# Row sums on one core: the head of the stream as two blocks of neighbouring rows with stores of their own, and the last group loaded whole

## The chip, the cores and the metric

The kernel runs on one core of a Trainium2 chip. The metric is the device time of one execution in microseconds (us), as the median of several runs. Three kinds of engine matter here. SyncE (SP) issues the loads and the last store. VectorE (DVE) and ScalarE (ACT) add the rows up, and ScalarE also issues stores. The core's 16 DMA engines move all the data.

## The reference

```python
x = np.random.randn(32, 512, 1024).astype(np.float32)

def reference(x):
    return np.sum(x, axis=-1).astype(np.float32)
```

There are 16384 rows of 1024 float32 numbers (67.1 MB in all), and each row gives one sum (64 KB in all).

## The kernel before

The rows are laid over 128 partitions, so a partition handles 128 rows. They are cut into eight groups (`last` = 7 is the number of the last one) of 2048 rows: in a group, partition p has 16 neighbouring rows, `BIG` = 16, so 64 KB of consecutive memory. The tile `sums` has 128 partitions and 128 columns, one column for each row of a partition. Column `j` belongs to group `j // 16`.

Input tiles come from a pool of three buffers. A load into a buffer waits until the sums of what was in it are done.

The work is in this order, written out by hand (`manual_schedule`):

1. The first 7 rows per partition of the *last* group are loaded into the first tile (`FIRST`, line 199). This load is moved to the very entry of the program by `issue_first_load_at_entry`. One DVE instruction (`vec`, line 141) makes its 7 sums. That instruction is named `first`.
2. Groups 0 to 6 follow, 16 rows per partition in one load each (lines 201 to 208). Groups 0 to 5 are summed by one DVE instruction each. Of group 6, DVE sums 9 rows one by one (`halves`, line 155: it adds the two halves of a row and accumulates) and ScalarE 7 (`act`, line 168). The load of group 1 is held until `first` is done (line 208).
3. The other 9 rows of the last group come in falling pieces: 6 rows (4 on DVE, 2 on ScalarE), 2 rows (one on each; the load is named `two`), and one row in two pieces of 560 and 464 numbers (`pieces`), both on DVE (lines 210 to 226).
4. ScalarE's queue issues one store of the sums of groups 0 to 6 (line 224), held until the load `two` has landed. SP issues the store of the last group's sums at the very end (line 227).

Two more helpers act when the program is finished. `order_waits` sets which of several waits comes first in an instruction. `wait_for_the_store_at_the_clear` takes the wait for the last store by SP out of SP's waits at the end of the program and puts it on GpSimd's clearing of the semaphores; SP's waits for all other DMAs, ScalarE's store among them, stay where they are, ahead of the engines' last meeting.

Of the kernel before, what the change touches and what calls it, by code (L numbers as in the profile page):

```python
# [100 lines left out]
@with_exitstack  # L101
def kernel(
    ctx: ExitStack,
    tc: tile.TileContext,
    x: bass.AP,
    out: bass.AP,
):
    nc = tc.nc
    nc.at_finalize(issue_first_load_at_entry)
    nc.at_finalize(order_waits)  # L110
    nc.at_finalize(wait_for_the_store_at_the_clear)
    fp32 = mybir.dt.float32
    P = 128
    batch, seq, dim = x.shape
    rows = batch * seq
    J = rows // P
    BIG = 16


    x_g = x.flatten_outer_dims().rearrange("(g p j) d -> g p j d", p=P, j=BIG)  # L120
    out_v = out.rearrange("b s -> (b s)").rearrange("(g p j) -> p g j", p=P, j=BIG)

    def rows_from(j, n):
        return x_g[j // BIG, :, j % BIG : j % BIG + n, :]

    last = J // BIG - 1
    FIRST = 7
    pieces = (560, 464)  # L130

    with (
        tc.tile_pool(name="in", bufs=3) as inpool,
        tc.tile_pool(name="unread", bufs=4, space=bass.MemoryType.PSUM) as upool,
        tc.tile_pool(name="stage", bufs=1) as stpool,
        tc.manual_schedule(),
    ):
        sums = stpool.tile([P, J], fp32)

        def vec(dst, src):  # L140
            return nc.vector.tensor_reduce(  # L141
                out=dst, in_=src, axis=mybir.AxisListType.X, op=mybir.AluOpType.add
            )

        def hold(inst, until, reason):
            tc.add_manual_dep(
                inst.ins,
                until.ins.name,
                mybir.DependencyInfo(mybir.DependencyClass.Sync, mybir.DependencyReason.DATA),
                reason=reason,  # L150
            )

        def halves(dst, src):
            n = src.shape[-1] // 2
            return nc.vector.tensor_tensor_reduce(  # L155
                out=src[:, :n],
                in0=src[:, :n],
                in1=src[:, n:],
                scale=1.0,
                scalar=0.0,  # L160
                op0=mybir.AluOpType.add,
                op1=mybir.AluOpType.add,
                accum_out=dst,
            )

        def act(dst, src, n):
            unread = upool.tile([P, dim], fp32)
            nc.scalar.activation(  # L168
                out=unread[:, :n],
                in_=src,  # L170
                func=mybir.ActivationFunctionType.Copy,
                accum_out=dst,
            )

        sums_of = []

        def rows(t, a, n, j, n_act, pairs=False):
            nv = n - n_act
            block = t[:, a * dim : (a + n) * dim].rearrange("p (n d) -> p n d", d=dim)
            load = nc.sync.dma_start(out=block, in_=rows_from(j, n))  # L180
            if pairs:
                for q in range(nv):
                    sums_of.append(halves(sums[:, j + q : j + q + 1], block[:, q, :]))
            else:
                sums_of.append(vec(sums[:, j : j + nv], block[:, :nv, :]))
            for q in range(nv, n):
                act(sums[:, j + q : j + q + 1], block[:, q, :], dim)
            return load

        def store(eng, g0, g1):  # L190
            return eng.dma_start(
                out=out_v[:, g0:g1],
                in_=sums[:, g0 * BIG : g1 * BIG].rearrange("p (g j) -> p g j", j=BIG),
            )


        j = last * BIG
        t = inpool.tile([P, BIG * dim + 4], fp32)
        rows(t, 0, FIRST, j, 0)
        first = sums_of[-1]  # L200
        for g in range(last):
            t = inpool.tile([P, BIG * dim + 4], fp32)
            if g < last - 1:
                load = rows(t, 0, BIG, g * BIG, 0)
            else:
                rows(t, 0, BIG, g * BIG, 7, pairs=True)
            if g == 1:
                hold(load, first, "no descriptors of later loads while the first ones start")

        t = inpool.tile([P, BIG * dim + 4], fp32)  # L210
        rows(t, FIRST, 6, j + FIRST, 2, pairs=True)
        two = rows(t, FIRST + 6, 2, j + FIRST + 6, 1, pairs=True)
        a = BIG - 1

        j += a
        c, width = pieces
        whole = t[:, a * dim + c : BIG * dim + 2]
        nc.vector.memset(whole[:, width + 1 :], 0.0)  # L220
        part = t[:, a * dim : a * dim + c]
        nc.sync.dma_start(out=part, in_=rows_from(j, 1)[:, 0, :c])  # L222
        nc.sync.dma_start(out=whole[:, 1 : width + 1], in_=rows_from(j, 1)[:, 0, c:])
        hold(store(nc.scalar, 0, last), two, "its packets come behind those of the loads")
        halves(whole[:, :1], part)
        halves(sums[:, j : j + 1], whole)
        store(nc.sync, last, last + 1)


# [28 lines left out]
```

## Time and profile before

| what | value |
|---|---|
| device time, median of 3 runs | 161.91 us (161.54 to 161.96) |
| span of the profiled execution, first to last instruction | 159.9 us |
| DVE busy | 120.6 us (75%) |
| ScalarE busy | 12.0 us (8%) |
| DMA queue of SP (q1): packets, bytes, share of the 16 engines' span | 1872, 67.12 MB, 97.7% |
| DMA queue of ScalarE (q10): the same | 912, 0.06 MB, 0.4% |

The profile is of one execution, and it gives that execution's span only, not a device time of its own. The median of the runs is 2.0 us above the span; those 2.0 us lie outside the first and the last instruction. Times within the profile are counted from the start of the span, which is the issue of the first load. "Landing" is when the semaphore of a DMA shows that all its data has arrived. A packet, in this kernel's DMAs, is what one partition gets or gives.

### The profile page before, as it was taken

What the parts mean: (1) busy time and instruction counts of PE and PEld (TensorE: products, weight loads), DVE (VectorE), ACT (ScalarE), POOL (GpSimd) and SP (SyncE); (2) the same over time, 40 slices, a digit from 0 to 9 for tenths busy, and PEclk for the clock granted to TensorE, in tenths of its full rate; (3) what the DMA queues carried; (4) which work ended last, traced back from release to release, by engine and by line L of the source; (5) the groups of instructions that cost most, each with busy time, mean ns of one, the idle gap of its engine ahead of it and who ended that gap; (6) DMA issues with size and microseconds to landing.
All of it is one profiled execution on the core that took longest, in us unless ns stands there. A gap on an engine that the chain in (4) does not pass through costs nothing.

```text
span 159.9 us, 132 instructions
## 1 busy us (share of the span) xinstructions
DVE 120.6 (75%) x40; ACT 12.0 (8%) x21; POOL 0.2 (0%) x4
## 2 busy tenths in 40 slices
DVE  0029600499985999779995899949999499994955
ACT  3000000000000000000000000000000000003993
POOL 0000000000000000000000000000000000000000
DMA  8899899799699699699699699799898996996994
GB/s 308 380 492 525 361 426 525 328 459 525 295 492 525 262 525 525 262 525 525 262 525 508 279 525 476 312 525 410 377 525 361 426 525 262 525 525 289 400 384 124
DMA packets 2784, 67.18 MB, mean 420 GB/s; under 512 B 1248, under 2 KB 1376, under 8 KB 1504
## 3 DMA queue, kind: packets, MB, share of 16 engines
q1 hardware_dynamic: 1872, 67.12, 97.7%
q10 hardware_dynamic: 912, 0.06, 0.4%
HBM read 67.11 MB, written 0.07 MB: 420 GB/s over the span
## 4 chain that ended last, share of the span: by engine, by line
DMA 71%; DVE 27%; SPq 1%; issue 0%; DVEq 0%
DMA t<-in_x_dram 71%; DVE sums L141 26%; SPq L180 0%; SPq L222 0%; DVE t L155 0%; DVEq L253 0%
## 5 line engine op out<-in xcount | busy, mean ns | idle before, releaser
L141 DVE TENSOR_REDUCE sums<-t 128x16 f32<-128x16384 f32 (+1 forms) x7 | 110.9, 15848 | 33.4 <-DMA t<-in_x_dram 33.4
L168 ACT ACTIVATE unread<-t 128x1024 f32<-128x1024 f32 x10 | 10.1, 1013 | 144.7 <-DMA t<-in_x_dram 144.7
L155 DVE CUSTOM_DVE_ANT_0 t<-t 128x512 f32<-128x512 f32 (+2 forms) x16 | 9.6, 654 | 4.1 <-DMA t<-in_x_dram 4.0
L168 ACT ACTIVATION_READ_ACCUMULATOR unread<-t 128x1 f32 x10 | 1.9, 188 | 0.0
L168 ACT ACT_TABLE_LOAD x1 | 1.3, 1283 | 0.8 <-PEq L242 0.8
L155 DVE DVE_READ_ACCUMULATOR2_ANT sums<- 128x1 f32 x15 | 1.2, 81 | 0.0
L242 POOL MEMSET const-bfloat16-1.0<- 128x1 bf16 x1 | 0.1, 102 | 0.0
L242 POOL MEMSET const-uint8-127<- 128x1 uint8 x1 | 0.1, 102 | 0.0
L242 POOL MEMSET const-float32-1.0<- 128x1 f32 x1 | 0.1, 99 | 0.0
L242 POOL MEMSET const-float32-0.0<- 128x1 f32 x1 | 0.1, 98 | 0.2 <-issue 0.2
L155 DVE DVE_READ_ACCUMULATOR2_ANT t<- 128x1 f32 x1 | 0.1, 83 | 0.0
L220 DVE MEMSET t<- 128x1 f32 x1 | 0.1, 59 | 0.0
## 6 DMA issues: line engine op xcount, KB each, us to landing
t<-in_x_dram SPq DMA_DIRECT2D x1, 3584.0 KB, 11.0
t<-in_x_dram SPq DMA_DIRECT2D x1, 3072.0 KB, 28.9
t<-in_x_dram SPq DMA_DIRECT2D x1, 1024.0 KB, 31.0
t<-in_x_dram SPq DMA_DIRECT2D x1, 280.0 KB, 31.2
t<-in_x_dram SPq DMA_DIRECT2D x1, 232.0 KB, 31.3
t<-in_x_dram SPq DMA_DIRECT2D x7, 40.8
out_dram<-sums ACTq DMA_DIRECT2D x1, 56.0 KB, 2.1
out_dram<-sums SPq DMA_DIRECT2D x1, 8.0 KB, 1.4
```

What stands on the lines that cost most here:

```text
L141: return nc.vector.tensor_reduce(out=dst, in_=src, axis=mybir.AxisListType.X, op=mybir.AluOpType.add)
L155: return nc.vector.tensor_tensor_reduce(out=src[:, :n], in0=src[:, :n], in1=src[:, n:], scale=1.0, scalar=0.0, op0=mybir.AluOpType.add, op ...
L168: nc.scalar.activation(out=unread[:, :n], in_=src, func=mybir.ActivationFunctionType.Copy, accum_out=dst,)
L220: nc.vector.memset(whole[:, width + 1 :], 0.0)
L242: nc = _bacc.Bacc("TRN2", target_bir_lowering=False, num_devices=1)
```

## The change

Rows 0 to 2047 (what was group 0) become two blocks, each laid over the partitions by itself: rows 0 to 895 with 7 neighbouring rows per partition (`HEAD`), and rows 896 to 2047 with 9. Both are loaded first, into one tile, by two loads, and each is summed by one DVE instruction. ScalarE's queue stores the 7 sums and then the 9 sums of each partition, each as soon as they are there. Groups 1 to 6 are loaded and summed as before. The last group is now loaded whole at the end: in pieces of 8 rows (5 on DVE, 3 on ScalarE), 5 (3 and 2), 2 (1 and 1), and the one row in pieces of 560 and 464. The late store on ScalarE's queue has groups 1 to 6 alone. It is held until `two`, and `two` is now the DVE sum of the first of the two rows, where it was the load of both.

```diff
+    HEAD = 7
...
+    def block_of(j):
+        if j < HEAD:
+            return 0, HEAD
+        if j < BIG:
+            return HEAD, BIG - HEAD
+        return j // BIG * BIG, BIG
 
     def rows_from(j, n):
-        return x_g[j // BIG, :, j % BIG : j % BIG + n, :]
+        first, size = block_of(j)
+        block = x_r[first * P : (first + size) * P, :].rearrange("(p j) d -> p j d", j=size)
+        return block[:, j - first : j - first + n, :]
...
-            return load
+            return load, summed
...
+        def store_block(eng, j):
+            first, size = block_of(j)
+            return eng.dma_start(
+                out=out_r[first * P : (first + size) * P].rearrange("(p j) -> p j", j=size),
+                in_=sums[:, first : first + size],
+            )
...
-        j = last * BIG
         t = inpool.tile([P, BIG * dim + 4], fp32)
-        rows(t, 0, FIRST, j, 0)
-        first = sums_of[-1]
-        for g in range(last):
+        _, first = rows_in(t, 0, HEAD, 0, 0)
+        rows_in(t, HEAD, BIG - HEAD, HEAD, 0)
+        store_block(nc.scalar, 0)
+        store_block(nc.scalar, HEAD)
+        for g in range(1, last):
             t = inpool.tile([P, BIG * dim + 4], fp32)
             if g < last - 1:
-                load = rows(t, 0, BIG, g * BIG, 0)
+                load, _ = rows_in(t, 0, BIG, g * BIG, 0)
             else:
-                rows(t, 0, BIG, g * BIG, 7, pairs=True)
+                rows_in(t, 0, BIG, g * BIG, 7, pairs=True)
             if g == 1:
                 hold(load, first, "no descriptors of later loads while the first ones start")
 
         t = inpool.tile([P, BIG * dim + 4], fp32)
-        rows(t, FIRST, 6, j + FIRST, 2, pairs=True)
-        two = rows(t, FIRST + 6, 2, j + FIRST + 6, 1, pairs=True)
+        j = last * BIG
+        rows_in(t, 0, 8, j, 3, pairs=True)
+        rows_in(t, 8, 5, j + 8, 2, pairs=True)
+        _, two = rows_in(t, 13, 2, j + 13, 1, pairs=True)
...
-        hold(store(nc.scalar, 0, last), two, "its packets come behind those of the loads")
+        hold(
+            nc.scalar.dma_start(
+                out=out_r[BIG * P : last * BIG * P].rearrange("(g p j) -> p g j", p=P, j=BIG),
+                in_=sums[:, BIG : last * BIG].rearrange("p (g j) -> p g j", j=BIG),
+            ),
+            two,
+            "its packets come behind those of the loads",
+        )
         halves(whole[:, :1], part)
         halves(sums[:, j : j + 1], whole)
-        store(nc.sync, last, last + 1)
+        store_block(nc.sync, last * BIG)
```

More of the change, by code (lines that the diff above doesn't have):

```diff
@@ L117 @@
     BIG = 16
-    x_g = x.flatten_outer_dims().rearrange("(g p j) d -> g p j d", p=P, j=BIG)
-    out_v = out.rearrange("b s -> (b s)").rearrange("(g p j) -> p g j", p=P, j=BIG)
+    HEAD = 7
+    last = J // BIG - 1
+    pieces = (560, 464)
+    x_r = x.flatten_outer_dims()
+    out_r = out.rearrange("b s -> (b s)")
+    def block_of(j):
[4 more added lines that the diff above has]
+        return j // BIG * BIG, BIG
     def rows_from(j, n):
-        return x_g[j // BIG, :, j % BIG : j % BIG + n, :]
-    last = J // BIG - 1
-    FIRST = 7
-    pieces = (560, 464)
+        first, size = block_of(j)
+        block = x_r[first * P : (first + size) * P, :].rearrange("(p j) d -> p j d", j=size)
+        return block[:, j - first : j - first + n, :]
     with (
@@ L173, in act, with rows_in @@
             )
-        sums_of = []
-        def rows(t, a, n, j, n_act, pairs=False):
+        def rows_in(t, a, n, j, n_act, pairs=False):
             nv = n - n_act
@@ L182, in rows @@
                 for q in range(nv):
-                    sums_of.append(halves(sums[:, j + q : j + q + 1], block[:, q, :]))
+                    summed = halves(sums[:, j + q : j + q + 1], block[:, q, :])
             else:
-                sums_of.append(vec(sums[:, j : j + nv], block[:, :nv, :]))
+                summed = vec(sums[:, j : j + nv], block[:, :nv, :])
             for q in range(nv, n):
                 act(sums[:, j + q : j + q + 1], block[:, q, :], dim)
-            return load
-        def store(eng, g0, g1):
+            return load, summed
+        def store_block(eng, j):
+            first, size = block_of(j)
             return eng.dma_start(
-                out=out_v[:, g0:g1],
-                in_=sums[:, g0 * BIG : g1 * BIG].rearrange("p (g j) -> p g j", j=BIG),
+                out=out_r[first * P : (first + size) * P].rearrange("(p j) -> p j", j=size),
+                in_=sums[:, first : first + size],
             )
-        j = last * BIG
         t = inpool.tile([P, BIG * dim + 4], fp32)
-        rows(t, 0, FIRST, j, 0)
-        first = sums_of[-1]
-        for g in range(last):
+        _, first = rows_in(t, 0, HEAD, 0, 0)
[3 more added lines that the diff above has]
+        for g in range(1, last):
             t = inpool.tile([P, BIG * dim + 4], fp32)
             if g < last - 1:
-                load = rows(t, 0, BIG, g * BIG, 0)
+                load, _ = rows_in(t, 0, BIG, g * BIG, 0)
             else:
-                rows(t, 0, BIG, g * BIG, 7, pairs=True)
+                rows_in(t, 0, BIG, g * BIG, 7, pairs=True)
             if g == 1:
```

## The prediction

> **What bounds the kernel now.** I read the page first, for the share of the DMA queues; then the timeline around the loads' landings, to see whether the stream of loads ever pauses; then the trace's packet records, for the price of a packet; last the timeline and the instructions of the program's end.
>
> ```profile
> DVE 120.6 (75%) x40; ACT 12.0 (8%) x21; POOL 0.2 (0%) x4
> ...
> q1 hardware_dynamic: 1872, 67.12, 97.7%
> q10 hardware_dynamic: 912, 0.06, 0.4%
> ```
>
> The loads' queue (q1) keeps the 16 DMA engines busy for 97.7% of the span: the bytes bound this kernel, not DVE at 75%.
>
> ```profile
> 11.03 7.62 DVE L141 TENSOR_REDUCE sums<-t 128x7 f32<-128x7168 f32 x1 [11.03 <-DMA t<-in_x_dram]
> 30.34 17.22 DVE L141 TENSOR_REDUCE sums<-t 128x16 f32<-128x16384 f32 x1 [11.69 <-DMA t<-in_x_dram]
> 49.69 17.22 DVE L141 TENSOR_REDUCE sums<-t 128x16 f32<-128x16384 f32 x1 [2.14 <-DMA t<-in_x_dram]
> ...
> 127.09 17.22 DVE L141 TENSOR_REDUCE sums<-t 128x16 f32<-128x16384 f32 x1 [2.13 <-DMA t<-in_x_dram]
> ...
> 156.36 1.03 ACT L168 ACTIVATE unread<-t 128x1024 f32<-128x1024 f32 x1 [0.30 <-DMA t<-in_x_dram]
> 156.37 0.69 DVE L155 CUSTOM_DVE_ANT_0 t<-t 128x512 f32<-128x512 f32 x1
> 156.45 0.41 ACTq L191 DMA_DIRECT2D out_dram<-sums  x1
> 156.98 0.08 DVE L155 DVE_READ_ACCUMULATOR2_ANT sums<- 128x1 f32 x1
> ...
> 157.69 0.40 DVE L155 CUSTOM_DVE_ANT_0 t<-t 128x233 f32<-128x233 f32 x1
> 158.02 0.08 DVE L155 DVE_READ_ACCUMULATOR2_ANT sums<- 128x1 f32 x1
> 158.13 0.35 SPq L191 DMA_DIRECT2D out_dram<-sums  x1
> ```
>
> Columns: start, length, engine, line, what, and in brackets the idle time before it and what ended it. A new group starts every 19.35 us, also the very first one behind the 7 rows (30.34 - 11.03 = 19.31), and a group costs DVE 17.22, so DVE waits 2.13 each time: the stream has no pause from its first packet (1.02 us, by the packet records) to its last (157.24). Only three stretches can be shortened or lengthened by anything but bytes: the 1.02 before the first packet, the 2.6 after the last one, and whatever is put into the stream between.
>
> **The price of a packet.** By the trace's packet records a load packet of 65536 bytes takes 2418 ns, of 28672 bytes 1062, of 8192 bytes 309. The first two give 36864 bytes in 1356 ns, 27.19 bytes per ns, and 1062 - 28672 / 27.19 = 7.5 ns per packet on top. A DMA over 128 partitions gives each engine 8 packets and a semaphore packet of 9 ns. For the stores, the DMA view of the window from 157.3 to 158.3 us has ScalarE's store alone:
>
> ```profile
> DMA packets 912, 0.06 MB, mean 57 GB/s; under 512 B 912, under 2 KB 912, under 8 KB 912
> ...
> q10 hardware_dynamic: 912, 0.06, 56.4%
> ```
>
> 0.564 us on each of 16 engines for 912 packets is 9.9 ns a packet; from the first to the last, 157.40 to 158.13, it is 0.73 us for 57 per engine, 12.8 ns with the gaps.
>
> **Loads.** The bytes are the same; 12 loads become 13 (7, 9, six of 16, 8, 5, 2 and two parts of a row). One more load: 8 x 7.5 + 9 ns = **+0.07 us** in the stream.
>
> **The two early stores.** Each gives each engine 8 packets (28 and 36 bytes) and one semaphore packet. They come at about 19 and 32 us, in the middle of the stream, so what they occupy is added to it: 18 packets x 9.9 to 12.8 ns = 0.18 to 0.23, I take **+0.20 us**. Nothing in this trace shows a small store between large loads, so zero (it fits into gaps) and more (first rival) stay open. On ScalarE's queue they wait for DVE until 18.66 and about 31.7; behind them stand its table load, if it comes after them, and its first sum, due at about 138, so that wait is covered by 106 us.
>
> The Trainium skill speaks against this part: DMA: Bandwidth & Descriptors, Rules for kernel authors, says of many small transfers "Coalesce into one large transfer; under 64 KB you're paying mostly overhead", and its section on the anatomy of one DMA has a fixed cost of about 2.0 us for each (for DMAs from GpSimd). By that, three more DMAs would be +6 us if they stood in line. The rows above say that an engine is held for some 10 ns per packet, and the rest of the 1.4 us from the last store's issue to its landing is latency, for which nothing here waits.
>
> **The order of the head.** DVE gets its first 7 rows at 11.0 as before. The hold on the second 16-row load is released at 18.66 as before; what covers it is less: 9 rows instead of 16. Nine rows are 8 packets of 36864 bytes, 8 x (1356 + 7.5) = 10.91 us; the engines end the first load between 10.14 and 10.64, so they run dry between 21.05 and 21.55. Issued at 18.68, the held load's first packet comes 0.85 to 1.02 later by the other DMAs' rows (up to 1.55 on the last engine for the first load): 19.5 to 20.2. Margin 0.8 or more; cost nothing. If ScalarE's first store, released by the same sum, were served ahead of it, its 0.41 of issue leaves 0.4. Later the third 16-row load waits for the 9-row sum: landing at 21.9, 9.75 us of DVE (1.067 per row and 0.15, from 17.22 and 7.62), 31.7, while two loads, to about 60, are still queued. Cost nothing. The rest of the groups run 8.4 us earlier against the stream, each still faster than its load.
>
> **The tail.** Group 6 lands at about 138 and takes ScalarE 7 x 1.04; 8 rows later, 9.7 us, the next piece. 5 DVE sums x 0.615 end long before the 5 rows land (about 153.9, where the 6 rows did); 3 sums then end 0.6 before the 2 rows land, where 4 ended just with it. From there the chain is the same: the last piece's landing (157.62), 0.40 of sum, store, landing at 159.56. Nothing gained, since the landing already was the last to come.
>
> **The late store.** Its hold moves from the load `two` to a DVE sum of it, which ended at 157.06. With 0.03 from a DVE result to the issue (158.10 to 158.13) and up to 0.08 for ScalarE's own waits, it is issued at 157.09 to 157.17 instead of 156.45: +0.64 to +0.72, less 0.10 for 8 of 57 packets. It landed at 158.58, by the semaphore records, so now at 159.12 to 159.20. SP checks that semaphore in its round of waits at the end, at 158.60, second of five, just after the landing; so this cover is gone. From the check to the meeting's end was 0.62; then GpSimd clears the semaphores when the last store has landed, at 159.59. With the check in its old place the meeting would end at about 159.8 and the clear move by 0.2 to 0.3; as the last of the five checks (0.43 before the meeting's end) by 0.0 to 0.1. The order is not visible in this profile; I take the middle, **+0.15 us**.
>
> Sum: 0.07 + 0.20 + 0.15 = +0.42, on a span of 159.88 and so on the median: 161.91 + 0.42 = **162.33 us**, taking the 2.0 us outside the span as unchanged. With the low ends +0.26, with the high ones 0.07 + 0.23 + 0.30 = +0.60. About 0.3%, 0.49 us, is what a measurement of this kernel can tell from no change.
>
> **Rivals.**
> 1. *Switching* (slower). A small store between large loads may cost an engine not 10 ns a packet but a fresh start of its stream. Row: the first packets of the first load took 1673 ns on average, the next ones 1062, so a start costs 0.61. One start: 0.42 + 0.61 = +1.03, 162.9; one for each store: +1.64, 163.55. It decides from 0.07 us for both beyond my 0.20. For it: no row excludes it, as no store of this trace lies between loads. Against: the semaphore packets between two loads cost 9 ns and no start. Chance 0.17.
> 2. *The end's high side* (slower). The late store's check stays early in SP's round: the sum is +0.49 to +0.60, 162.45. Chance 0.21.
> 3. *Starving head* (slower). The held load's first packet needs over 2.4 us from its issue. Every us beyond costs one, and a start of 0.61: at 3 us, +0.42 + 0.6 + 0.6, 163.5. All three issue rows speak against it. Chance 0.05.
> 4. *Faster head.* Seven neighbouring rows in one stretch, instead of 28 KB out of each 64 KB, might read faster at the start: at most the 0.61 of the first packets, and with free stores and no late meeting 0.07 - 0.61 = -0.54, 161.4. Against: 24576-byte packets with the same 64 KB pitch took 912 ns, as the line above gives (911). Chance 0.07. [...]
> 5. *It does nothing.* Stores and end hidden: +0.07, 162.0, within 0.3%; chance 0.06.
>
> **How the numbers follow.** My forecast, the sum between +0.26 and +0.49, has 0.44 (its own range 162.1 to 162.4). Same is 0.44 + 0.06 = 0.50; slower 0.17 + 0.21 + 0.05 = 0.43; faster 0.07. The range reaches down to 161.8 (rival 5, and runs that differ by 0.4) and up to 163.3, between one and two starts; outside are rival 4 and the upper half of rivals 1 and 3, 0.07 + 0.11 = 0.18.
>
> **What would show it.** Right: loads still without a pause, the 16-row sums 19.35 apart, the first of them at about 41.3; the last piece landing at 157.8 to 158.0 (157.62 + 0.27); ScalarE's late store issued 0.6 to 0.7 after the `two` rows land; the clear 0.0 to 0.3 later against that landing. Wrong: a gap of the DMA engines near 21 us (rival 3), 16-row steps at 21 or 41 us longer by more than 0.3 (rival 1), a first landing before 10.7 (rival 4).

## The result and the profile after

The changed kernel takes 162.07 us (161.78 to 162.44, 9 runs), the kernel before 161.58 in 9 runs beside it (161.50 to 161.96). The ratio on record is 1.0025, with a 95% interval from 1.0015 to 1.0036: 0.40 us slower, between 0.24 and 0.58 (the two medians alone lie 0.49 apart). That is clear of zero. The estimate is below 0.3%, as forecast, but the interval reaches to 0.36%, and the prediction gave this 0.50 against 0.43 for slower. 162.07 lies in its range.

The base of the forecast was off. The three runs that the prediction started from had a median of 161.91; by the longer series before is at 161.6 to 161.7. The 2.0 us that the text before and the prediction put outside the span come from setting that median against the span of another execution: in every run here whose span is on record the time is 1.7 to 1.9 us above its own span. So the profile before, with its span of 159.88, belongs to a time of about 161.65, and 161.65 + 0.42 is 162.07.

The page of the changed kernel, its DMA queues (packets, MB, share of the 16 engines' span):

```profile
q1 hardware_dynamic: 2016, 67.12, 97.5%
q10 hardware_dynamic: 1072, 0.06, 0.4%
```

The queue of the loads is as full as before; there are 144 packets more on it (one load) and 160 more on ScalarE's queue (two small stores, with their semaphore packets, less the 128 that the late store lost).

The timeline of the changed kernel, for the head, the first 16-row groups and the end:

```profile
11.17 7.62 DVE L147 TENSOR_REDUCE sums<-t 128x7 f32<-128x7168 f32 x1 [11.17 <-DMA t<-in_x_dram]
18.82 13.41 ACTq L197 DMA_DIRECT2D out_dram<-sums  x2
22.09 9.75 DVE L147 TENSOR_REDUCE sums<-t 128x9 f32<-128x9216 f32 x1 [3.30 <-DMA t<-in_x_dram]
...
41.46 17.22 DVE L147 TENSOR_REDUCE sums<-t 128x16 f32<-128x16384 f32 x1 [9.62 <-DMA t<-in_x_dram]
60.82 17.22 DVE L147 TENSOR_REDUCE sums<-t 128x16 f32<-128x16384 f32 x1 [2.14 <-DMA t<-in_x_dram]
80.19 17.22 DVE L147 TENSOR_REDUCE sums<-t 128x16 f32<-128x16384 f32 x1 [2.15 <-DMA t<-in_x_dram]
...
156.60 0.69 DVE L161 CUSTOM_DVE_ANT_0 t<-t 128x512 f32<-128x512 f32 x1 [0.57 <-DMA t<-in_x_dram]
157.22 0.08 DVE L161 DVE_READ_ACCUMULATOR2_ANT sums<- 128x1 f32 x1
157.25 0.06 DVE L225 MEMSET t<- 128x1 f32 x1
157.33 0.39 ACTq L230 DMA_DIRECT2D out_dram<-sums  x1
...
157.94 0.40 DVE L161 CUSTOM_DVE_ANT_0 t<-t 128x233 f32<-128x233 f32 x1
158.27 0.08 DVE L161 DVE_READ_ACCUMULATOR2_ANT sums<- 128x1 f32 x1
158.38 0.35 SPq L197 DMA_DIRECT2D out_dram<-sums  x1
```

The stream has no pause: 9 rows are 10.92 behind 7, and the 16-row groups are 19.36 apart, though small stores lie between them. What is lost in the loads shows at two places: the first sum starts 0.14 later (11.17 against 11.03), the last one 0.25 (157.94 against 157.69). The late store is issued at 157.33, 0.73 after the two rows' sums began; before it was 0.08.

SP's queue, who it waited for (total, times, longest, us), in the changed kernel:

```profile
SPq L265 <- PEq L265: 0.6, 2, 0.5
SPq L197 <- DVE sums L161: 0.6, 1, 0.6
SPq L265 <- DMA out_dram<-sums: 0.4, 1, 0.4
```

The last line is new: at the program's end SP now stands 0.4 us for a store. It is the late store, which lands at 159.32 by the semaphore records. GpSimd's clear then starts 0.11 behind the landing of the last store (159.91 and 159.80); in the kernel before it was 0.02. So the span's +0.33 (160.20 against 159.88) is +0.12 at the end of the first load (10.76 and 10.65, slowest engine), +0.12 in the stream behind it, and +0.09 at the end.

### The profile page after: what moved, and what is told of

The parts are those of the page before. It is cut to its first block, busy times and chain, and to the rows that moved or that the text cites. A ratio compares the mean times of both kernels' runs of the same rounds, so it can differ in the third digit from the quotient of the medians.

```text
span 160.2 us, 150 instructions
## 1 busy us (share of the span) xinstructions
DVE 115.7 (72%) x48; ACT 15.2 (10%) x27; POOL 0.2 (0%) x4
## 4 chain that ended last, share of the span: by engine, by line
DMA 71%; DVE 27%; SPq 1%; issue 0%; DVEq 0%
DMA t<-in_x_dram 71%; DVE sums L147 26%; SPq L185 1%; SPq L227 0%; DVE t L161 0%; DVEq L265 0%
## 5 line engine op out<-in xcount | busy, mean ns | idle before, releaser
L147 DVE TENSOR_REDUCE sums<-t 128x16 f32<-128x16384 f32 (+2 forms) x7 | 103.5, 14782 | 32.6 <-DMA t<-in_x_dram 32.6
L174 ACT ACTIVATE unread<-t 128x1024 f32<-128x1024 f32 x13 | 13.2, 1013 | 110.2 <-DMA t<-in_x_dram 110.2
L161 DVE CUSTOM_DVE_ANT_0 t<-t 128x512 f32<-128x512 f32 (+2 forms) x20 | 12.2, 663 | 10.0 <-DMA t<-in_x_dram 9.8
L174 ACT ACTIVATION_READ_ACCUMULATOR unread<-t 128x1 f32 x13 | 2.4, 187 | 0.0
```

The lines of the kernel that those rows point to most:

```text
L147: return nc.vector.tensor_reduce(out=dst, in_=src, axis=mybir.AxisListType.X, op=mybir.AluOpType.add)
L161: return nc.vector.tensor_tensor_reduce(out=src[:, :n], in0=src[:, :n], in1=src[:, n:], scale=1.0, scalar=0.0, op0=mybir.AluOpType.add, op ...
L174: nc.scalar.activation(out=unread[:, :n], in_=src, func=mybir.ActivationFunctionType.Copy, accum_out=dst,)
```

## The experiments

The comparisons are with the kernel before on the same chip; its medians there were 161.65 to 161.69. The theory: one more load +0.07, the early stores something up to 0.2, the late store's hold +0.09. The rivals: the hold is hidden; the stores are free, or cost far more; the addresses of the head count.

**e1: the hold taken back.**

```diff
-        _, two = rows_in(t, 13, 2, j + 13, 1, pairs=True)
+        two, _ = rows_in(t, 13, 2, j + 13, 1, pairs=True)
```

> The changed kernel with one edit taken back: the late store is held until the load of the two rows has landed, not until DVE's sum of the first of them. Theory (the sum of the prediction: stream +0.25, end +0.09): the store is issued some 0.65 us sooner, lands near 158.8, SP's check of it (fourth of five) does not wait, and GpSimd's clear comes 0.03 us behind the landing of the last store instead of 0.11. Time 0.09 us less than the changed kernel: before +0.2 to +0.3. Rival (the end hides the late store, all of the loss is in the stream): no difference to the changed kernel, +0.33 to +0.45 against before. Rival (the store's packets then run into the last loads): the last load's landing later by up to 0.5 us, slower than the changed kernel.

Measured: 162.05 us, ratio 1.0022 (1.0013 to 1.0032). The late store is issued at 156.81 and lands at 158.78, SP's line of waiting for a store is gone, and the clear is 0.02 behind the last landing: the mechanism is as said. The time does not settle 0.09: against the changed kernel it is -0.05, within the interval.

**e2: the hold alone, in the kernel before.**

```diff
-        two = rows(t, FIRST + 6, 2, j + FIRST + 6, 1, pairs=True)
+        rows(t, FIRST + 6, 2, j + FIRST + 6, 1, pairs=True)
+        two = sums_of[-1]
```

> The kernel before with this edit alone: the late store is held until DVE's sum of the first of the two rows. In this kernel SP checks the late store second of five, so the prediction's high end applies: the store lands near 159.2, SP's check waits some 0.5 us for it, the clear comes 0.2 to 0.3 us behind the last store's landing. Theory: +0.2 to +0.27 us against before, with the last load's landing unchanged at 157.6. Rival (the end hides it): 0.0.

Measured: 162.04 us, 1.0020 (1.0009 to 1.0030), +0.32. SP's queue in e2:

```profile
SPq L254 <- DMA out_dram<-sums: 0.7, 1, 0.7
SPq L254 <- PEq L254: 0.6, 2, 0.5
```

SP checks this store second of five, stands 0.7 us, and the clear starts 0.41 behind the last store's landing, with the last load at 157.61 as before. The hold by itself costs +0.38 in this profile, more than the 0.2 to 0.3 expected: from the store's landing (159.22) to the clear (159.94) it takes 0.72. The 0.62 of the prediction ends with the meeting; the clear came some 0.1 after that.

The same hold is worth 0.09 in the changed kernel, 0.29 less, for two reasons of about the same size. There SP checks the store fourth of five, so from the check to the clear it is 0.58 and not 0.71. And the store, six groups instead of seven, lands 0.48 before the last store, in e2 only 0.32 before it.

**e3: no early stores.** The sums of rows 0 to 2047 are not written.

```diff
-        store_block(nc.scalar, 0)
-        store_block(nc.scalar, HEAD)
```

> The changed kernel without the two early stores (the sums of rows 0 to 2047 stay in the tile and are not written). The check of the late store moves from fourth to third of five, worth up to +0.07 at the end. By the packets' price (18 packets of 10 to 13 ns in the stream): last landing 0.18 to 0.23 us sooner than in the changed kernel, time 0.1 to 0.2 less. By the spacing of the landings in the profile of the changed kernel (six 16-row steps with the stores between them take 116.14 us, 116.16 without): the stores cost nothing, last landing the same, time 0.0 to +0.07. Rival (a fresh start of the stream for each store): over 0.6 less.

Measured: 162.17 us, 1.0026 (1.0015 to 1.0038). Nothing is saved that the time can show. The check of the late store is third here, and in this profile the clear comes 0.19 behind the last landing instead of 0.11, so some 0.08 of a saving would be hidden by the end, and the time alone does not exclude 0.2. The landings do; they stand with e4.

**e4: five more early stores.**

```diff
                 load, _ = rows_in(t, 0, BIG, g * BIG, 0)
+                store_block(nc.scalar, g * BIG)
...
-                out=out_r[BIG * P : last * BIG * P].rearrange("(g p j) -> p g j", p=P, j=BIG),
-                in_=sums[:, BIG : last * BIG].rearrange("p (g j) -> p g j", j=BIG),
+                out=out_r[(last - 1) * BIG * P : last * BIG * P].rearrange("(g p j) -> p g j", p=P, j=BIG),
+                in_=sums[:, (last - 1) * BIG : last * BIG].rearrange("p (g j) -> p g j", j=BIG),
```

> The changed kernel with the sums of groups 1 to 5 stored by ScalarE's queue too as soon as they are there (five more early stores of 64 bytes per partition), and the late store with group 6 alone (8 packets per engine instead of 48). By the packets' price: 45 more packets per engine in the stream, +0.45 to +0.58 us in the last landing; the late store lands some 0.5 us sooner, so the end's 0.09 goes: +0.35 to +0.5 against the changed kernel. If small packets between large ones are free: last landing unchanged, time 0.09 less than the changed kernel. Rival (a fresh start of 0.61 for each store): +3 us.

Measured: 162.06 us, 1.0024 (1.0014 to 1.0035). With the end's 0.09 back, five stores cost 0.07, some 0.25 either way, not 0.45 to 0.58. The timeline of e4 has the reason in view; each of these groups had a small store among its packets:

```profile
41.85 17.22 DVE L147 TENSOR_REDUCE sums<-t 128x16 f32<-128x16384 f32 x1 [9.64 <-DMA t<-in_x_dram]
61.23 17.22 DVE L147 TENSOR_REDUCE sums<-t 128x16 f32<-128x16384 f32 x1 [2.15 <-DMA t<-in_x_dram]
80.58 17.22 DVE L147 TENSOR_REDUCE sums<-t 128x16 f32<-128x16384 f32 x1 [2.13 <-DMA t<-in_x_dram]
99.95 17.22 DVE L147 TENSOR_REDUCE sums<-t 128x16 f32<-128x16384 f32 x1 [2.15 <-DMA t<-in_x_dram]
```

The steps are 19.38, 19.35 and 19.37, against 19.36 in the changed kernel and 19.35 before: at most 0.03 us for a store.

The semaphore records have it finer. From the landing ahead of the six 16-row loads to the landing of the sixth it is 116.11 us in e2, e3 and e6, which have no small store there (116.16 in the kernel before, some of whose packets were slow in that execution), 116.13 to 116.14 with two of them (the changed kernel, e1, e10), and 116.24 with those of e4. That is 0.01 to 0.02 us for a store. In the packet records, large packets start 2.420 us apart on an engine with a small one between them, and 2.414 without.

**e7: the 9-row block first.** Only `HEAD = 7` becomes `HEAD = 9`.

> The changed kernel with the blocks exchanged in size: 9 rows first and then 7 (HEAD = 9). The hold on the next load then ends with the 9-row sum: landing near 13.4, 9.75 us of sum, 23.2, first packet near 24.2; the 7 rows that cover it run out between 21.05 and 21.55 as before. Theory (the cover of the hold is what the prediction says): a gap of some 2.7 to 3.1 us in the stream, +2.7 to +3.7 us against the changed kernel with the fresh start of the engines. Rival (something else keeps the engines fed, or the hold does not matter): no difference.

Measured: 165.99 us, 1.0278 (1.0254 to 1.0303): 3.9 over the changed kernel by the medians, 4.1 by the ratios. A table of windows of e7 (window, length, busy DVE, ScalarE, GpSimd, clock, DMA share, GB/s) shows the gap:

```profile
20.00:21.00 1.00, 1.00 (x1) 0.00 (x0) 0.00 (x0) 1.00 1.06 459
21.00:22.00 1.00, 1.00 (x1) 0.00 (x0) 0.00 (x0) 1.00 0.01 0
22.00:23.00 1.00, 1.00 (x1) 0.00 (x0) 0.00 (x0) 1.00 0.00 0
23.00:24.00 1.00, 1.00 (x2) 0.00 (x0) 0.00 (x0) 1.00 0.00 0
24.00:24.50 0.50, 0.50 (x1) 0.00 (x0) 0.00 (x0) 1.00 0.00 0
24.50:25.00 0.50, 0.50 (x1) 0.00 (x0) 0.00 (x0) 1.00 5.07 1704
```

(A packet counts in the window in which it starts.) The held load is issued at 23.55, its first packet starts 0.97 later, and the first packets take 0.65 us longer than later ones. The engines had run out between 21.1 and 21.9, so each stood still for some 3.4 us, and 3.4 + 0.65 is about what was measured. The mechanism is as expected; the size is over the expected 3.7, since the first 9 rows landed at 13.75 and not at 13.4.

**e10: no hold on the load of group 1.**

```diff
-            if g == 1:
-                hold(load, first, "no descriptors of later loads while the first ones start")
```

> The changed kernel without the hold on the load of group 1 (it is issued at about 1.1 us, not at 18.8). The profiles with the hold have two or three packets at 21.1 us that took 154 to 454 ns more than 2418: the first packets of the load that had been held. Theory (cover enough, the engines that end last are not touched): no difference to the changed kernel, +0.3 to +0.5 against before, the packets at 21 us at 2418. Rival (the shorter cover costs something): up to 0.3 us less than the changed kernel. Rival (what the hold is there for, by the name that the code gives it, descriptors of later loads disturb the start): the first load ends later than 10.8 to 11.2, slower.

Measured: 162.10 us, 1.0021 (1.0012 to 1.0030): no difference that can be told from the changed kernel's 1.0025. The packets at 21 us are back at 2418 ns, and the first load ends at 10.93, inside the span of the others. With 7 rows first, the cover of 9 is enough.

**e8: ten loads for five** (with the hold of e1).

```diff
-                load, _ = rows_in(t, 0, BIG, g * BIG, 0)
+                load, _ = rows_in(t, 0, 8, g * BIG, 0)
+                rows_in(t, 8, 8, g * BIG + 8, 0)
```

> As e1 (late store held until the load of the two rows), and groups 1 to 5 loaded as two loads of 8 rows each and summed by two DVE instructions each: five loads more. Theory (7.5 ns for each packet and 9 for a semaphore packet): +5 x 0.069 = +0.35 us against e1, so +0.65 to +0.75 against before. Rival (the packet's extra time is hidden when the next one is already waiting): no difference to e1. Rival (each load costs far more than its packets): +1 us or more.

Measured: 162.31 us, 1.0040 (1.0028 to 1.0053), against 1.0022 of e1: about +0.3 for five loads, some 0.25 either way, 0.35 expected. The timeline of e8:

```profile
61.23 8.69 DVE L147 TENSOR_REDUCE sums<-t 128x8 f32<-128x8192 f32 x1 [1.03 <-DMA t<-in_x_dram]
70.94 8.69 DVE L147 TENSOR_REDUCE sums<-t 128x8 f32<-128x8192 f32 x1 [1.03 <-DMA t<-in_x_dram]
80.65 8.69 DVE L147 TENSOR_REDUCE sums<-t 128x8 f32<-128x8192 f32 x1 [1.03 <-DMA t<-in_x_dram]
```

Two steps of 9.71 are 19.42 for 16 rows, 0.06 over 19.36, as the price of a packet has it. The load's term stands.

**e6, e5, e11, e9: the addresses of the head.** The profiles up to e4 suggested that packed rows start slower. e6 packs the first load of the kernel before:

```diff
+    x_r = x.flatten_outer_dims()
     def rows_from(j, n):
+        if n == 7:
+            return x_r[j * P : (j + 7) * P, :].rearrange("(p j) d -> p j d", j=7)
```

> The kernel before with its first load alone packed: the 7 rows of a partition come from 896 neighbouring rows (14336 to 15231) instead of 28 KB out of each 64 KB. The rest reads what it read before, so some rows of the last group are added up twice and others not at all; the work and all sizes are those of the kernel before. Theory H: +0.15 to +0.3 us against before, the first load ending at 10.8 to 11.2. Rival (addresses do not matter): 0.0, first load ending near 10.7.

Measured: 161.89 us, 1.0009 (0.9999 to 1.0018), +0.15 and not quite clear of zero; the first load ends at 11.04, late as the theory has it.

e5 unpacks the head of the changed kernel:

```diff
         first, size = block_of(j)
+        if first < BIG:
+            first, size = 0, BIG
...
+            part = out_r[first * P : (first + size) * P].rearrange("(p j) -> p j", j=size)
+            if first < BIG:
+                part = out_r[: BIG * P].rearrange("(p j) -> p j", j=BIG)[:, first : first + size]
+            return eng.dma_start(out=part, in_=sums[:, first : first + size])
```

> The changed kernel, with the 7 and the 9 rows of a partition taken from its 16 neighbouring rows of group 0, as in all other groups: so 28 KB and 36 KB out of each 64 KB of memory, not packed blocks; the two early stores write 28 and 36 bytes out of each 64. Nothing else differs. Theory H (the packed first block starts slower: in the profiles so far its slowest first packet took 2319 to 2676 ns with packed rows and 1935 and 2161 without, and the slowest engine ended the first load at 10.76 to 11.18 us against 10.65 and 10.71): the first load ends near 10.7 and the time falls by 0.15 to 0.3 against the changed kernel, to +0.1 to +0.25 against before. Rival (the addresses do not matter; the first packets differ by chance): no difference to the changed kernel, +0.4.

Measured: 162.35 us, 1.0043 (1.0030 to 1.0055): 0.3 over the changed kernel, with intervals that just overlap, where the theory said faster and the rival the same. Neither fits. e11 unpacks the first load alone (`if first < HEAD` in place of `if first < BIG`, in `rows_from` only):

> The changed kernel with its first load alone in 64 KB steps: the 7 rows of a partition come from 28 KB out of each 64 KB of group 0; the 9 rows stay a packed block. Some of the first 2048 rows are added up twice and others not at all; work and sizes are those of the changed kernel. Theory H (a packed first block starts slower by 0.1 to 0.3): first load ends at 10.65 to 10.71, time 0.1 to 0.3 less than the changed kernel, +0.1 to +0.3 against before. Rival (as in e5): first load ends early, the time goes up all the same, +0.5 to +0.7 against before, so the early end brings the slow stretch. Rival (addresses do not matter): +0.4.

Measured: 162.21 us, 1.0024 (1.0013 to 1.0036): as the changed kernel. The first load ends early (10.70), but nothing is gained. e9 is e5 with the edit of e1:

> e5 and e1 together: the head in 64 KB steps, and the late store held until the load of the two rows. So of the change only one more load and the two early stores in the middle of the stream are left. e5's profile had the first load end early (10.67), and then lost 0.7 us between 60 and 120 us, where its 16-row packets took up to 206 ns more than 2418. Theory C (that loss comes by chance of the runs): the sum of what is left is +0.08 for the load and near 0 for the stores, so +0.05 to +0.15 against before, and no slow stretch. Rival (the head in 64 KB steps followed by this order brings the slow stretch every time): +0.5 to +0.7 against before, slow packets between 60 and 120 us again.

Measured: 162.34 us, 1.0032 (1.0018 to 1.0046), +0.52 (0.29 to 0.74): the rival's +0.5 to +0.7, and not theory C. The timeline of e9 has a slow stretch again:

```profile
60.96 17.22 DVE L149 TENSOR_REDUCE sums<-t 128x16 f32<-128x16384 f32 x1 [2.17 <-DMA t<-in_x_dram]
80.50 17.22 DVE L149 TENSOR_REDUCE sums<-t 128x16 f32<-128x16384 f32 x1 [2.32 <-DMA t<-in_x_dram]
100.06 17.22 DVE L149 TENSOR_REDUCE sums<-t 128x16 f32<-128x16384 f32 x1 [2.34 <-DMA t<-in_x_dram]
```

Steps of 19.54 and 19.56 instead of 19.36: two 16-row loads lost 0.2 us each, in packets that took longer than 2418 ns. The packet records of all profiles, by how the first load reads (e7 left out):

| first load | profiles | its slowest engine ends at | from there to the last packet |
|---|---|---|---|
| packed | after, e1, e3, e4, e6, e8, e10 | 10.76 to 11.18, mean 10.96 | 146.5 to 147.0 |
| 64 KB steps, a 16-row load behind it | before, e2 | 10.65, 10.71 | 146.6, 146.5 |
| 64 KB steps, the 9 rows behind it | e5, e9, e11 | 10.67 to 10.72 | 147.1 to 147.5 |

So the late first end with packed rows is in all seven profiles, by 0.27 on average. (The profiles of e4 and e8, with 11.18 and 11.04, are of the longest run of their series; without them it is 0.21.) The cost of it in the time is only bounded: e6 has 0.15, from nothing to 0.29. And the slow stretch came in all three profiles of the third kind, at different places between 60 and 140 us, and took back more than the early end gave. Those three profiled executions (162.63, 162.71, 162.39) were longer than the medians of their series (162.35, 162.34, 162.21), so they may show it larger than usual. What makes these packets slow is open.

## Why the prediction was right, and where it was not

*The total* is right: +0.42 forecast, +0.40 (0.24 to 0.58) measured. Its terms are not all right: the early stores were priced too high, a late end of the first load was not in the sum, and the two errors cancel. That the sum came out so close is luck. (Its low end, 0.07 + 0.18 + 0.0, is 0.25 and not 0.26.)

*One more load, +0.07*: right. e8's five loads cost about 0.3, its steps 0.06 each.

*The early stores, +0.20*: this is the term that was mis-sized. By the landings the two cost 0.02 to 0.03 together; the time of e3 and e4 agrees within some 0.25. The step that failed is "what they occupy is added to" the stream: it took the 9.9 ns that a packet occupies for time that the loads lose. In an engine's records a small packet lies between two large ones and puts the start of the next one off by only 6 ns, and over whole loads even less is lost. Rival 1, a fresh start for a store, fell with it. The +6 us for DMAs that stand in line fell too. The Trainium skill's rule on small transfers (DMA: Bandwidth & Descriptors, Rules for kernel authors), "under 64 KB you're paying mostly overhead", does not describe what these stores cost the stream: one of 3.5 KB does take long to land (22.8 us, below), but nothing waits for it.

*The late store, +0.15 with 0.0 to 0.3*: the mechanism was right, link by link: issue after DVE's sum, landing, SP's round of waits, the clear. In the changed kernel it is 0.09 in the profile, with the check fourth of five, a place between the two ends that were priced; the time of e1 is too coarse to settle that, but e2's +0.32 (0.15 to 0.49) shows that such a wait is paid for. The high end was too low: 0.38 in e2, where the prediction left out the time from the meeting's end to the clear.

*The order of the head, 0 for the cover*: right. (The load that is held is the second 16-row load in the kernel before, but the first in the changed one; the 9 rows of cover are counted rightly.) e10 shows that the hold costs nothing that can be told with 7 rows first, and e7 that with 9 it leaves a gap of 3.4 us.

*The head's addresses, 0, with a gain of up to 0.61 as rival 4*: wrong in sign. The row given against rival 4 (912 ns at a 64 KB pitch) is of packets in mid-stream; the difference is in the first packets, which took 1758 to 1878 ns on average in the seven profiles with packed rows and 1606 to 1724 in the five without. So the packed block does not start faster; its first load ends 0.27 later on average, 0.12 later in the pair of profiles shown above. What that adds to the time is between 0 and 0.29 (e6). With 0.07 for the load, 0.03 for the stores and 0.09 for the end it makes 0.19 to 0.48, which holds the measured 0.40; the runs do not settle it closer, since e5, e9 and e11, meant to take it away, brought a loss of their own.

*The tail's new pieces, 0*: as forecast, the sums of the 5 rows ended 0.57 before the 2 rows landed, and the chain from there was unchanged.

No version ran faster than the kernel before.

## What to carry to other kernels

When the DMA engines are busy from the first packet to the last, an edit is worth what it puts into that stream and what it does to the two ends; count packets of loads, and follow each store's semaphore to the instruction that waits for it last. In these runs a store that nobody waited for cost 0.01 to 0.02 us in the stream of large loads. A store shortly before the end is paid for if it lands late and its wait stands early in a serial round of checks (0.38 us in e2, 0.09 here), so both belong in the estimate. A load that is held needs cover for the sum it waits for and about 1 us to its first packet: exchanging 7 and 9 rows costs about 4 us. And set a profile's span against the time of its own run, not against the median of others.

## What the hardware showed that was not expected

A small store issued while large loads are queued lands very late. The DMA view of the changed kernel (size, us from issue to landing):

```profile
out_dram<-sums ACTq DMA_DIRECT2D x1, 48.0 KB, 2.0
out_dram<-sums ACTq DMA_DIRECT2D x1, 3.5 KB, 22.8
out_dram<-sums ACTq DMA_DIRECT2D x1, 4.5 KB, 29.1
out_dram<-sums SPq DMA_DIRECT2D x1, 8.0 KB, 1.4
```

3.5 KB took 22.8 us, and 48 KB at the end of the loads 2.0. The records show why: the store's 8 packets on an engine go one at a time between load packets of 2418 ns, from 23.4 to 41.0 us. In e8, with load packets of half the size, the same 8 packets went from 22.3 to 31.7. The Trainium skill has this rule: DMA: Bandwidth & Descriptors, Queues, rings and completion order, says that an engine takes turns between its queues packet by packet. The records agree.

A late engine seems to stay late. Each of the 16 engines ends a load with a semaphore packet. Between the first and the last of these 16 there were, for the first load, 0.50 us in the kernel before, 0.70 in the changed kernel, 0.91 in e1 and 1.12 in e4; for the last load, 146 us later, there were 0.40, 0.70, 0.73 and 0.93. (The records do not name the engine, so that it is the same one is not shown.) Executions of one kernel differ by 0.3 to 0.8 us (1.0 in e7); how much of that comes from the first load is not shown.
